# A decoder layer whose second-phase weights wait on a store: other places for two weight tiles and one raw tile

## The chip, the cores and the metric

The kernel runs on one core of a Trainium2 chip. The metric is the device time of one execution in microseconds. It is written in a tile language: the program names tiles from pools, and a planner sets the order of the instructions in each engine's queue, gives the tiles their places and adds the waits. Each engine then works through its own queue in that order.

## The reference

One hybrid decoder layer on 1024 tokens of width 1024, in float32:

```
h = x + W_out( concat[ NSA attention, retention ] )     # both read rmsnorm(x) @ W_in
y = h + W_down( relu(rmsnorm(h) @ W_up)^2 )             # W_up 1024 x 4096, W_down 4096 x 1024
```

Only the last line matters here. All products keep full float32 accuracy by splitting each operand into a rounded high part and the remaining low part; a product is three TensorE products (high x high, high x low, low x high).

## The kernel before

The last part of the kernel computes the line with W_up and W_down by a block scheme with seven products in place of eight (a Winograd-like scheme): weights and activations are cut into two by two blocks, and sums of blocks are multiplied.

**First phase** (`up(p)`, lines 1097 to 1187, p = 0 to 15). Each p is a pair of 128-wide slices of the 4096. It forms seven products (named by the weights 11, 12, S2, S1, S3, S4, 22) and from them the blocks u11, u12, u22, u21 after relu and square, in temporary tiles of the pool `fp`, tag `tmp`, 11 places of 2 KB per partition. From those it makes seven sums, kept as split tiles (`keep`, line 1117: k0, k5, k3, k4, k2, k1, k6 in that order). For p up to 14 a kept tile lies in one of the places hac2 to hac7 (hac4 to hac7 for p = 13 and 14) and is stored to HBM as dU by a DMA that POOL issues; for p = 15 it stays in SBUF. The pair's weight operands lie in the places wo8 to wo11, for p = 14 in hac0 to hac2, for p = 15 in hac0 to hac3.

**Second phase** (lines 1303 to 1400). Eight groups g of two pairs each, and in each group two halves c of the output columns. For each (g, c) seven products n, each of 2 x 6 TensorE products of 128 x 512: in the first block (g = 0, c = 0) in the order 0, 3, 5, 2, 4, 1, 6. Group 0 is pairs 0 and 15. The weights of W_down are loaded raw, four sums are made of them by VectorE, and each of seven is split: ScalarE casts the high part (line 1005), VectorE subtracts to get the low part (line 175).

**The first weights** (`first_w`, lines 1264 to 1291) are prepared beside pair 15. `first_w` is a generator; it is moved one step on before pair 15's sums and at each of the yields of `up(15)`: its raw tiles take wo8 to wo11; after u11 is kept, it splits weights 0, 3 and 5 into `tmp` tiles; after u12 and u22 are copied out of PSUM (lines 1169 and 1172), weights 2 into hac6 and 1 into hac2; after the sums, 4 into hac7 and 6 into hac3. In the call put(n, i) a number i means the place hac i, and none means two `tmp` tiles. hac2 and hac3 last held weights of pair 15; hac6 and hac7 last held k4 and k2 of pair 14.

**The later weights** (`later_w`, lines 1322 to 1329) take raw tiles wq (14 KB per partition) and split tiles wh and wl, two of each, from the pool `fd`, which is opened when the pools of the first phase are closed and lies over their places. A tile of `fd` waits for the last users of what lay there. From low to high: the "T1" and "T4" blocks, "12"/"T3", "22", then the raw tiles of the first weights (wo8 to wo11), small temporaries, and the "11", "21" and "T2" blocks. Tiles of `fd` are laid out in the order in which the program names them first: wh, wl, wh, wl, then wq, then eleven places u10, u9, u8, u7, u0 to u6 of 4 KB each, into which the kept tiles are loaded back from dU. SP issues those loads, POOL those of wq.

The planner plans with its own times; an instruction whose tile has no free place yet is passed over and others of its engine come first. Places of one tag are given out in the order in which the tiles are named.

Of the kernel before, what the change touches and what calls it, by code (L numbers as in the profile page):

```python
# [11 lines left out]
F32 = mybir.dt.float32  # L12
F32R = mybir.dt.float32r
# [88 lines left out]
def hybrid_layer(ctx, tc, xT, x, wfm, wv, vecs, pe, w1, w2, w_out, w_up, w_down,  # L102
# [901 lines left out]
    def split(to, raw):  # L1004
        nc.scalar.copy(to[0], raw)  # L1005
        sub_lo(to[1], raw, to[0])
# [42 lines left out]
    places = {"raws": raws, "ma": ma}  # L1049
# [197 lines left out]
    def load_w(g, c, parts, q=nc.gpsimd):  # L1247

        cols = slice(256 * c, 256 * c + 256)
        for k, p in enumerate(pairs[g]):  # L1250
            for i, to in enumerate(parts):
                q.dma_start(to(k), w_down[2 * p + i].rearrange("p (h n) -> p h n", h=2)[:, :, cols])  # L1252

    def sums_w(b):

        minus(b[3], b[4], b[6], ALU.add)
        minus(b[2], b[3], b[0])
        minus(b[4], b[0], b[4])
        minus(b[5], b[1], b[2])
# [4 lines left out]
    def first_w():  # L1264

        t = [fw.tile([128, 2, 2, 256], F32, name=f"wq0{i}", tag=f"wo{8 + i}") for i in range(4)]
        load_w(0, 0, [lambda q: t[0][:, :, q], lambda q: t[1][:, :, q]], nc.sync)
        b = {n: t[i][:, j].rearrange("p q n -> p (q n)")
             for i, ns in enumerate(((0, 4), (1, 6), (3, 2), (5,))) for j, n in enumerate(ns)}
        yield  # L1270

        def put(n, i=None):
            if i is None:
                w0[n] = [fp.tile([128, 512], F32R, name=f"w0{n}{j}", tag="tmp", bufs=11) for j in range(2)]
            else:
                to = hs.tile([128, 2, 512], F32R, name=f"w0{n}", tag=f"hac{i}")
                w0[n] = [to[:, 0], to[:, 1]]
            split(w0[n], b[n])

        sums_w(b)  # L1280
        for n in (0, 3, 5):
            put(n)
        yield
        put(2, 6)
        put(1, 2)
        yield
        put(4, 7)
        put(6, 3)
        yield
        yield  # L1290

    sums, w0 = norm(), {}
    for p in range(1, NU):
        fetch_up(p + 1)
        ahead = first_w() if p == NU - 1 else itertools.repeat(None)
        next(ahead)
        sums_up(p)
        for _ in up(p):
            next(ahead)
        first_up(p + 1)  # L1300
        if p >= 4:
            next(sums, None)
    ups.close()

    with ExitStack() as s1:
        fd = s1.enter_context(tc.tile_pool(name="fd", reuse_waits="tile", bufs=1))
        dx, dy, dz = Ring("DX"), Ring("DY"), Ring("DZ")

        def wide(n, g, c, dtype=F32R):
            return fd.tile([128, 7, 2, 256], dtype, name=f"{n}_{g}{c}", tag=n if n == "wq" else f"{n}{c}")  # L1310


        parts_w = {(g, c): [wide(n, g, c) for n in ("wh", "wl")] for g, c in ((1, 0), (0, 1))}
        raw_w = {(0, 1): wide("wq", 0, 1, F32)}
        places["fd"] = fd
        early = {k: fd.tile([128, 2, 512], F32R, name=f"u{'0' if k < 7 else '1'}{k}", tag=f"u{k}")
                 for k in (10, 9, 8, 7, 0, 1, 2, 3, 4, 5, 6)}
        for _ in range(11):
            next(spots)
        early = [early[k] for k in range(11)]  # L1320
# [53 lines left out]
        for g in range(NG):  # L1374
            for c in range(2):
# [10 lines left out]
                for n in ORDER if g or c else (0, 3, 5, 2, 4, 1, 6):  # L1386
                    ps = y if n in (3, 5) else z if n == 1 else x
                    for j in range(2):
# [3 lines left out]
                        else:  # L1392
                            k = 2 * c + j
# [119 lines left out]
```

## Time and profile before

| | us |
|---|---|
| median of three runs | 1305.87 |
| the three runs | 1301.57, 1305.87, 1306.34 |
| profiled execution | 1302.99 |
| its span | 1301.2 |
| TensorE busy | 1239.2 |
| VectorE busy | 997.7 |
| ScalarE busy | 684.2 |

The times stand on a scale from the span's start. The first phase of the last part runs from about 670 to 974 us, the second to the end. PE is TensorE, DVE VectorE, ACT ScalarE, POOL GpSimd, SP SyncE. A TensorE product's shown duration (0.39 us) overlaps the next one: what counts is the distance of starts. Tile names in rows leave numbers out: "w<-wq" is a cast of one of the first weights, "u<-px" the copy of u12, "k<-u" a kept tile, "dU<-k" its store.

### The profile page before, as it was taken

How to read it: one execution, taken by the hardware profiler on the slowest of the kernel's cores; microseconds unless marked ns; L12 is line 12 of the kernel's file. 1: busy time of each engine (PE TensorE's matmuls, PEld its weight loads, DVE VectorE, ACT ScalarE, POOL GpSimd, SP SyncE). 2: the span in 40 equal slices, each digit the busy share in tenths (PEclk: the TensorE clock that was granted, in tenths of full speed). 3: DMA queues.
4: the chain of work that ended last, by engine and by line, in shares of the span. 5: the costliest groups of instructions: out<-in, count | busy, mean ns of one | idle time of the engine just before them, and what ended most of it. 6: DMA issues, size and time to landing. Idle time of an engine off the chain costs nothing.

```text
span 1301.2 us, 19827 instructions
## 1 busy us (share of the span) xinstructions
PE 1239.2 (95%) x6682; PEld 1059.8 (81%) x6682; DVE 997.7 (77%) x2185; ACT 684.2 (53%) x1348; POOL 366.5 (28%) x551
## 2 busy tenths in 40 slices
PE   7999999799999999889989999999979999999898
PEld 6888878799999988677767888888767878878786
DVE  7685874588779886577798788887764687787887
ACT  7424412467788775454677787777664322112220
POOL 0344424555566463122101111211110111101010
PEclk9999999899999999999999999999989999999899
DMA  6477569212321531981326777777772578766563
GB/s 231 139 226 212 156 191 321 98 58 74 108 76 63 210 106 40 267 228 66 122 82 250 275 274 259 291 254 269 278 283 108 224 282 306 268 222 251 214 251 121
DMA packets 98805, 252.30 MB, mean 194 GB/s; under 512 B 12640, under 2 KB 30432, under 8 KB 98704
## 3 DMA queue, kind: packets, MB, share of 16 engines
q1 hardware_dynamic: 69488, 150.05, 35.3%
q0 software_dynamic: 29216, 100.98, 20.2%
q8 instruction: 53, 0.87, 0.3%
q14 instruction: 48, 0.39, 0.1%
HBM read 162.19 MB, written 88.74 MB: 193 GB/s over the span
## 4 chain that ended last, share of the span: by engine, by line
PE 32%; issue 12%; DVE 8%; DMA 5%; POOL 3%; ACT 2%; SPq 0%; POOLq 0%; DVEq 0%; ACTq 0%
PE dx L1348 4%; PE dx L1349 4%; PE dx L1347 4%; POOL dU L166 2%; PE dy L1347 2%; PE dy L1348 2%; PE dy L1349 2%; PE px L1106 2%; PE px L1108 2%; DMA rg<-dRG 2%; PE px L1107 2%; DVE y L1357 1%; PE dz L1347 1%; PE dz L1348 1%; PE dz L1349 1%
## 5 line engine op out<-in xcount | busy, mean ns | idle before, releaser
L166 POOL DMA_DIRECT2D dU<-k x105 | 56.0, 533 | 250.4 <-DVE k L175 250.1
L1252 POOL DMA_DIRECT2D wq<-in_w_down x60 | 42.5, 714 | 259.9 <-DVE wl L175 244.2
L1005 ACT CAST wh<-wq 128x1536 fp32r<-128x1536 f32 (+1 forms) x30 | 50.8, 1699 | 118.2 <-DVE wq L1009 99.2
L1347 PE MATMUL dx<-u,wh 128*128 128x512 f32 x232 | 90.0, 394 | 3.1 <-ACT wh L1005 1.6
L1348 PE MATMUL dx<-u,wl 128*128 128x512 f32 x232 | 91.2, 393 | 0.6 <-DVE wl L175 0.6
L175 DVE TENSOR_TENSOR tl<-pt,th 128x512 fp32r<-128x512 f32 (+2 forms) x136 | 80.2, 597 | 14.6 <-ACT th L784 14.0
L1349 PE MATMUL dx<-u,wh 128*128 128x512 f32 x232 | 90.3, 392 | 0.0
L1357 DVE TENSOR_TENSOR y<-dx,y 128x512 f32<-128x512 f32 x90 | 61.3, 687 | 30.9 <-PE dx L1349 28.2
L1005 ACT CAST k<-u 128x512 fp32r<-128x512 f32 x112 | 67.6, 622 | 30.9 <-DVE u L1009 29.2
L175 DVE TENSOR_TENSOR k<-u,k 128x512 fp32r<-128x512 f32 x112 | 76.3, 686 | 6.8 <-ACT k L1005 6.4
L784 ACT CAST th<-pt 128x512 fp32r<-128x512 f32 (+2 forms) x136 | 68.1, 515 | 22.6 <-PE pt L839 20.3
L839 PE MATMUL pt<-ident,p 128*128 128x128 f32 x456 | 71.8, 275 | 0.8 <-DVE sbias L707 0.5
L831 PE MATMUL po<-tl,v 128*128 128x256 f32 (+1 forms) x272 | 70.2, 293 | 0.8 <-DVE tl L175 0.8
L831 PE MATMUL po<-th,v 128*128 128x256 f32 (+1 forms) x272 | 68.6, 274 | 0.1
L1391 ACT COPY dz<-dx 128x512 f32<-128x512 f32 x32 | 18.3, 570 | 95.1 <-PE dx L1349 95.1
L775 POOL TENSOR_SCALAR p<-p,rs 128x896 f32<-128x896 f32 (+3 forms) x64 | 48.0, 749 | 48.3 <-DVE rs L773 20.5
L175 DVE TENSOR_TENSOR wl<-wq,wh 128x1536 fp32r<-128x1536 f32 (+1 forms) x30 | 60.3, 2017 | 0.4 <-ACT wh L1005 0.4
L759 ACT ACTIVATE p<-p,mn 128x896 f32<-128x896 f32 (+3 forms) x64 | 49.8, 778 | 13.7 <-DVE mn L752 13.0
L839 PEld LDWEIGHTS pt<-ident,p 128*128 128x128 f32 x456 | 52.4, 140 | 5.0 <-DVE tl L175 1.4
L1106 PE MATMUL px<-bhT,wS 128*128 128x512 f32 x120 | 47.7, 398 | 8.9 <-ACT u L1169 8.9
L1347 PEld LDWEIGHTS dx<-u,wh 128*128 128x128 f32 x232 | 43.8, 189 | 14.1 <-DVE y L1357 3.1
L831 PEld LDWEIGHTS po<-tl,v 128*128 128x128 f32 x272 | 51.5, 189 | 2.1 <-DVE tl L175 1.4
(514 smaller groups left out, 4306.7 us busy)
## 6 DMA issues: line engine op xcount, KB each, us to landing
dU<-k POOLq DMA_DIRECT2D x105, 512.0 KB, 3.6
u<-dU SPq DMA_DIRECT2D x105, 512.0 KB, 6.9
raw<-in_w_up SPq DMA_DIRECT2D x32, 512.0 KB, 4.3
wq<-in_w_down POOLq DMA_DIRECT2D x60, 256.0 KB, 5.1
xraw<-in_xT SPq DMA_DIRECT2D x16, 256.0 KB, 5.2
w1r<-in_w SPq DMA_DIRECT2D x32, 128.0 KB, 3.7
dQ<-stg_Q POOLq DMA_DIRECT2D x8, 512.0 KB, 5.6
q<-dQ SPq DMA_DIRECT2D x64, 64.0 KB, 2.4
```

The costliest lines, as they stand in the source:

```text
L166: return (q or nc.sync).dma_start(dst.bitcast(F32), src.bitcast(F32)).ins
L175: eng.tensor_tensor(lo, src, hi.bitcast(F32), op=ALU.subtract)
L759: nc.scalar.activation(buf[:, :n], buf[:, :n], AF.Exp, scale=-1.0, bias=mn[:, u, fin:fin + 1], accum_out=sm[:, 0, u, 0:1])
L784: nc.scalar.copy(th[:, :w], pt[:, :w])
L831: mm = nc.tensor.matmul(po[:, cs], vals[g, kt // 4][:, kt % 4, br], q[:, o:o + 128 * len(us)], start=False, stop=end and q is parts[1])
L839: nc.tensor.transpose(pt[:, o:o + 128], res[u][0][:, c:c + 128], ident)
L1005: nc.scalar.copy(to[0], raw)
L1106: nc.tensor.matmul(ps, wh[:, cs], bh, start=first and m == 0, stop=False, skip_group_check=not first)
L1347: nc.tensor.matmul(ps, wh[:, q, cs], u[:, 0], start=first and q == 0, stop=False, skip_group_check=not first)
L1348: nc.tensor.matmul(ps, wl[:, q, cs], u[:, 0], start=False, stop=False, skip_group_check=not first)
L1349: nc.tensor.matmul(ps, wh[:, q, cs], u[:, 1], start=False, stop=q == 1, skip_group_check=not first)
L1357: nc.vector.tensor_tensor(y, ps, y, op=ALU.add)
```

## The change

In `first_w` weights 2 and 4 are split into `tmp` tiles instead of hac6 and hac7, and the split of 4 is named one step earlier, behind that of 2. In the second phase the raw tile wq is named third of the rest, behind u10 and u9, where it was named first; so these two move 14 KB down and wq 8 KB up.

```
-        put(2, 6)
+        put(2)
+        put(4)
         put(1, 2)
         yield
-        put(4, 7)
         put(6, 3)
...
-        raw_w = {(0, 1): wide("wq", 0, 1, F32)}
-        places["fd"] = fd
-        early = {k: fd.tile([128, 2, 512], F32R, name=f"u{'0' if k < 7 else '1'}{k}", tag=f"u{k}")
-                 for k in (10, 9, 8, 7, 0, 1, 2, 3, 4, 5, 6)}
+        places["fd"], early, raw_w = fd, {}, {}
+        for k in (10, 9, 8, 7, 0, 1, 2, 3, 4, 5, 6):
+            if k == 8:
+                raw_w[0, 1] = wide("wq", 0, 1, F32)
+            early[k] = fd.tile([128, 2, 512], F32R, name=f"u{'0' if k < 7 else '1'}{k}", tag=f"u{k}")
```

## Rows read from the trace of the kernel before

**Rows 1.** The page: span, busy time of the engines.
```profile
span 1301.2 us, 19827 instructions
...
PE 1239.2 (95%) x6682; PEld 1059.8 (81%) x6682; DVE 997.7 (77%) x2185; ACT 684.2 (53%) x1348; POOL 366.5 (28%) x551
```

**Rows 2.** Waits of TensorE, whole run: us in total, times, longest us.
```profile
PE px L1106 <- ACT u L1169: 8.9, 2, 8.2
...
PE dy L1347 <- DVE y L1357: 3.1, 1, 3.1
...
PE dy L1347 <- ACT y L1355: 1.4, 1, 1.4
```

**Rows 3.** The chain that ended last, 940 to 1000 us: start, us, what.
```profile
954.85 8.31 DMA dU<-k
```

**Rows 4.** Timeline of ScalarE, 953 to 964.5 us: start, us, engine, line, operation.
```profile
957.20 1.12 ACT L1005 CAST w<-wq 128x512 fp32r<-128x512 f32 x2
958.23 0.63 ACT L1115 ACTIVATE u<-u 128x512 f32<-128x512 f32 x1
958.76 0.60 ACT L1005 CAST w<-wq 128x512 fp32r<-128x512 f32 x1
959.27 0.62 ACT L1005 CAST k<-u 128x512 fp32r<-128x512 f32 x1
959.79 0.62 ACT L1005 CAST w<-wq 128x512 fp32r<-128x512 f32 x1
963.18 0.62 ACT L1005 CAST w<-wq 128x512 fp32r<-128x512 f32 x1 [2.78 <-DMA dU<-k]
963.71 0.58 ACT L1169 COPY u<-px 128x512 f32<-128x512 f32 x1
```

**Rows 5.** Timeline of TensorE, 955 to 969 us.
```profile
955.53 0.39 PE L1107 MATMUL pz<-bl,w 128*128 128x512 f32 x1
955.76 0.39 PE L1108 MATMUL pz<-bh,w 128*128 128x512 f32 x1
964.34 0.79 PE L1106 MATMUL px<-bhT,wS 128*128 128x512 f32 x1 [8.19 <-ACT u L1169]
...
968.35 0.44 PE L1106 MATMUL px<-bhT,wS 128*128 128x512 f32 x1
```

**Rows 6.** Two other holes of TensorE; stretches beside them, third column from the end: granted clock.
```profile
238.80 0.58 PE L347 MATMUL a_RVA<-wh_RVA,xhi 128*128 128x256 f32 x1 [4.47 <-ACT gRG L356]
...
673.60 0.51 PE L1106 MATMUL pz<-bh,w 128*128 128x512 f32 x1 [2.69 <-ACT pz L1160]
...
238.00:245.00 7.00, 5.49 (x24) 5.19 (x24) 5.01 (x14) 2.04 (x5) 5.30 (x7) 0.51 0.31 95
...
675.00:678.00 3.00, 3.00 (x9) 2.32 (x8) 3.00 (x6) 1.84 (x3) 0.55 (x1) 0.50 0.67 274
```

**Rows 7.** Timeline of POOL, 950 to 1000 us.
```profile
972.05 2.88 POOL L1252 DMA_DIRECT2D wq<-in_w_down  x4 [14.65 <-PE py L1108]
999.64 0.71 POOL L1252 DMA_DIRECT2D wq<-in_w_down  x1 [24.70 <-DVE wl L175]
```

**Rows 8.** Stretches around these loads: the last two columns are DMA share and GB/s.
```profile
963.00:972.00 9.00, 7.66 (x25) 6.18 (x26) 1.98 (x3) 4.07 (x7) 0.00 (x0) 0.70 1.03 420
...
978.00:990.00 12.00, 10.56 (x47) 8.44 (x46) 3.95 (x7) 4.43 (x9) 0.00 (x0) 1.00 0.01 1
```

**Rows 9.** Timelines of ScalarE, VectorE and TensorE in the second phase's first block.
```profile
974.74 0.60 ACT L1114 ACTIVATE u<-px 128x512 f32<-128x512 f32 x1
...
991.81 2.01 DVE L1009 TENSOR_TENSOR wq<-wq 128x512 f32<-128x512 f32 x3
...
994.94 1.75 DVE L175 TENSOR_TENSOR wl<-wq,wh 128x1536 fp32r<-128x1536 f32 x1
...
995.97 0.61 PE L1347 MATMUL dx<-u,wh 128*128 128x512 f32 x2
...
996.75 0.50 PE L1348 MATMUL dx<-u,wl 128*128 128x512 f32 x1 [0.16 <-DVE wl L175]
```

## The prediction

> **What bounds the kernel now.** I read the page first [rows 1]: TensorE is busy for 95% of the span, so the time falls only where TensorE waits or runs slowly. The waits of TensorE over the whole run [rows 2] name the largest such place in one row: 8.2 us at one time, a product into px that waits for ScalarE's copy of u (line 1169). It is in the last pair of the first phase (p = 15). The chain that ended last [rows 3] says what stood behind it: from 954.85 us, for 8.31 us, the store of a kept product into dU; when it lands, ScalarE's cast of a first weight w starts. ScalarE's timeline [rows 4] shows the queue: the cast that waited 2.78 us for "DMA dU<-k" and directly behind it the copy of u for which TensorE waits. A queue in order holds the copy back, though the copy has nothing to do with the store. In the code the waiting cast is put(4, 7): its target hac7 was last the source of the store of k2 of pair 14. Of the two casts "x2" at 957.20 one is put(2, 6), into hac6, the source of k4's store, which has landed by then.
>
> TensorE's timeline [rows 5] gives the price. Products run 0.23 us apart (955.53, 955.76); the last one before the hole ends at 956.15, the next begins at 964.34. Nine products then take 964.34 to 968.35, 4.01 us, where 9 x 0.227 = 2.04 us is the usual time: 1.97 us more, because the granted clock is at 1.2 of its 2.4 GHz after the hole (mean 0.70 from 963 to 972 [rows 8]). The place costs 8.19 + 1.97 = 10.2 us in all.
>
> **The change part by part.**
>
> *put(2) and put(4) go to temporaries.* No instruction goes or comes; two casts and two subtracts get other targets. A "tmp" place is given out in the order in which the program names the tiles (11 places). Before, the six halves of weights 0, 3, 5 are named ahead of u12 and u22, and weights 2 and 4 used hac places, so that they could slip ahead of u12 on ScalarE. Now 2 and 4 are named behind u12 and u22 in the same ring and must come later. So ahead of the u12 copy there are left, from 957.20 on: the cast of 0, the square of u11, the cast of 3, the cast of k0, the cast of 5. ScalarE steps 0.52 us from one to the next when it waits for nothing (958.76, 959.27, 959.79 in [rows 4]). The copy starts at 957.20 + 5 x 0.52 = 959.80 instead of 963.71: 3.91 us earlier. That is the wait with its wake-up, 963.18 - (959.79 + 0.52) = 2.87 us, and two casts that now stand behind the copy, 1.04 us. TensorE resumes at about 960.43, and the hole is 4.28 us instead of 8.19. It does not close: the five instructions, and the relu of u11 ahead of them, remain. Bounds: -2.87 us if both casts are still ahead, -8.19 if the planner finds a way to copy u12 at once. I take -3.91.
>
> *The clock.* Holes of 4.47 us (ending at 238.80) and 2.69 us (ending at 673.60) are each in the neighbourhood of a stretch at half the granted clock: 238 to 245 at 0.51, 675 to 678 at 0.50 [rows 6]. A hole of 4.28 us lies between these two. Beside the first the slow stretch covers some 6 us of work (a loss of 3.0), beside the second 3 us (1.5); now it is 1.97. So bounds +1.0 and -0.5, and -1.97 if no slow stretch came; I take 0: a hole that is only halved still pays.
>
> *What is now short: the ring.* Pair 15 needs u11, u12, u22, u21 and ten halves of weights, 14 tiles in 11 places. The halves of 4 get their places only when u11 and u12 are used up, and u21 one when the first product of the second phase (n = 0) has used weight 0. Times, all moved by 3.9: pair 15's last product ends at about 970.6, n = 0 takes 12 x 0.227 = 2.7 us, so the relu of u21 starts at about 973.5, against 974.74 before [rows 9]. It was late already: nothing is lost against it. k1 and k6, made from u21, are first read at n = 1 and n = 6, the last in the order 0, 3, 5, 2, 4, 1, 6, and even n = 4 is 4 x 2.7 us away. Weight 4's split ends at about 975, six microseconds before n = 4. What can move is TensorE's wait of 1.4 us for the copies "y" (the row dy <- ACT y in [rows 2]), which stand on ScalarE behind the cast of k6. With u21 later the cast of k6 comes behind them: a gain up to 1.4; one more cast (weight 4) stands there: a loss up to 0.6, or 1.2 with its subtract's delay. I take -0.7.
>
> *The later weights' raw tile moves.* With u10 and u9 named first, wq takes 8 KB further on: it leaves the last quarter of the "22" blocks and lies over the raw tiles of the first weights. Its four loads on POOL (issued from 972.05 on, 2.88 us [rows 7]) wait for TensorE's S4 product and the raw splits before; now for the subtract of weight 4, at about 975. POOL has nothing else to issue until 999.64, so nothing is queued behind them. They are used by VectorE's sums from 991.81 on, and TensorE's first product with the later weights is at 995.97 [rows 9]; moved by 3.9 this is 987.9 and 992.1. The DMA engines are full until 972 (share 1.03) and idle from 978 on (0.01) [rows 8]: before, all four had landed 6 us after the first issue; so now at 981, 7 us ahead of the sums. Cost 0, bounds 0 and the shift that rival C prices. The Trainium skill ("DMA: Bandwidth & Descriptors", section "Issuing engines are not separate DMA queues") says that transfers started by different engines end up on the same 16 DMA engines and interleave; by that rule a load that meets SP's loads of the kept tiles could take the 8.3 us of the store in [rows 3] from its last issue and land at 986, 2 us ahead of the sums instead of 7, the sum still being what it is and rival C nearer. The share of 0.01 in [rows 8] speaks against such a meeting. u10 and u9 now wait for TensorE's S4 product and are read two groups later: 0.
>
> *Behind it* TensorE is dense: of the waits in [rows 2] the second phase has 3.1 us and smaller ones, so what is gained here is kept to the end unless the planner, which orders every engine's queue anew for the whole second phase, draws it otherwise. That I cannot read from a trace; the size of one such redrawn place is the row dy <- DVE y: 3.1 us and its slow clock.
>
> **Sum.** -3.9 + 0 - 0.7 + 0 = -4.6 us. The profiled execution took 1302.99 us (span 1301.2 and 1.8 around it): 1298.4. The median of the runs, 1305.87, is 2.9 above the profiled one; from it 1301.3. I name the middle, 1299.8.
>
> **The rivals.**
> A. *The hole closes.* ScalarE copies u12 ahead of the weights, and the slow clock goes with it: -10.2 us, from the middle base of 1304.4 to 1294.2. For it: the product that it copies stands ahead of pz's in TensorE's queue, and pz's is through at the hole's start. Against it: the order of the names, which keeps six halves of weights ahead of u12.
> B. *Nothing is gained.* The ring of 11 is too short in practice: the planner puts u21's relu ahead of the cast of k3 on ScalarE, both stand until n = 0 is through, and n = 3 waits for relu, square, cast [rows 4] and subtract (2.01 us for three in [rows 9]), 0.6 + 0.6 + 0.6 + 0.7 = 2.5 us, and the y copies 1.4 more: -3.9 + 3.9 = 0, 1304.4. For it: 14 tiles in 11 places. Against it: k3 is made by a subtract that waits neither for u21 nor for n = 0.
> C. *Slower.* The raw tile of the later weights comes free too late. The load needs 2.9 us to issue and about 3 to land, the sums to the first product 995.97 - 991.81 = 4.2, the first subtract 1.75 [rows 9]: some 12 us from issue to use. The second block needs it at 992.1, so up to an issue at 980 nothing shows, and each us beyond is one on the path. If weight 4's places come free only at the end of the first block (7 x 2.7 us after 970.6, at 989.6), TensorE stands until 1001.6, 9.5 us, and the sum is -3.9 + 9.5 = +5.6, with a slow clock of 1.5 to 3 behind the hole: +7 to +8.6, about 1312. For it: the last reader of that place is the very weight that now waits for a place. Against it: two places come free at about 973 with u11 and u12.
> D. *The planner's new order* makes or removes a later hole such as that of 3.1 us, with 1.5 to 3 us of slow clock: 5 to 6 us either way, 1294 or 1305.
>
> **How the numbers follow.** Likeliest 60%, A 9%, B 13%, C 5%, D 13%, half to each side. The likeliest's own range is -2 to -8 us (the bounds of the hole and the clock, and runs that lie 5 us apart among themselves), so a good fourth of it is beyond 0.5%, which is 6.5 us and about what a measurement here can tell from no change. Faster: 0.26 x 60 + 9 + 6 = 31%; slower: C and a little of D, 6%; the same: 63%. The range is 1293 to 1306.5: A and the good half of D at its low end, B and the bad half of D at its high end; C and the tails are left out.
>
> **What would show it.** Right: no cast of w on ScalarE waits for "DMA dU<-k"; the copies of line 1169 and 1172 follow directly on the cast of weight 5; TensorE's hole before S3 is 4 to 4.5 us and still has half a clock behind it; wq's load is issued near 975 and no product waits for wh or wl more than the 0.2 us of before. Wrong: a hole under 2 or over 6 us; a new wait of TensorE on k1, k3, w or wh in the 30 us behind pair 15; a change of the waits after 1000 us larger than that of the hole.

## The result, and the profile after

The changed kernel took 1295.48 us (median of 16 runs, 1292.81 to 1301.60), the kernel before beside it on the same chip 1303.88 us (16 runs, 1300.80 to 1307.58): a ratio of 0.9942, interval 0.9930 to 0.9954, so about 7.6 us less. The time lies inside the range of 1293.0 to 1306.5 and 4.3 us below the 1299.8 named. Of the three classes the one with the largest chance (within 0.5%, 63%) did not come; faster by over 0.5% (31%) did, by little. Run twice more, the changed kernel gave 0.9958 [0.9943, 0.9974] and 0.9948 [0.9930, 0.9966]: whether the gain is over 0.5% is not settled by these, that there is a gain is.

The profiled execution of the changed kernel took 1300.51 us, 5 above its median: its total says little here, and the places inside it say much. Its span is 1298.7 us. From the page, the busy times as in [rows 1]:

```profile
PE 1240.7 (96%) x6682; PEld 1062.0 (82%) x6682; DVE 997.8 (77%) x2185; ACT 684.1 (53%) x1348; POOL 366.0 (28%) x551
```

The work is the same; what went is waiting. TensorE's waits after (us in total, times, longest), against [rows 2]; the second phase's lines stand one further down in the code:

```profile
PE px L1106 <- ACT u L1169: 4.9, 2, 4.3
...
PE dy L1348 <- DVE y L1358: 3.1, 1, 3.1
...
PE dy L1348 <- DMA u<-dU: 2.1, 1, 2.1
```

The wait on line 1169's copy is 4.3 us instead of 8.2, the one on the copies y (1.4 us) has no row any more, that on VectorE's y is unchanged, and there is a new one on a load of a kept tile. ScalarE's timeline after shows the queue of [rows 4] without the store:

```profile
958.30 0.59 ACT L1114 ACTIVATE u<-pz 128x512 f32<-128x512 f32 x1
958.79 0.61 ACT L1005 CAST w<-wq 128x512 fp32r<-128x512 f32 x1
959.30 0.63 ACT L1115 ACTIVATE u<-u 128x512 f32<-128x512 f32 x1
959.83 0.60 ACT L1005 CAST w<-wq 128x512 fp32r<-128x512 f32 x1
960.34 0.62 ACT L1005 CAST k<-u 128x512 fp32r<-128x512 f32 x1
960.86 0.62 ACT L1005 CAST w<-wq 128x512 fp32r<-128x512 f32 x1
961.38 0.58 ACT L1169 COPY u<-px 128x512 f32<-128x512 f32 x1
961.85 0.59 ACT L1172 COPY u<-py 128x512 f32<-128x512 f32 x1
962.33 0.63 ACT L1005 CAST w<-wq 128x512 fp32r<-128x512 f32 x1
```

Between the relu of u11 and the copy stand exactly the five instructions of the prediction (the casts of 0, 3 and 5, a square, a kept tile's cast), none of them with a wait; weight 2's cast comes behind both copies. TensorE's timeline after, the place of [rows 5], and under it stretches of the same trace (columns: length, busy time and count of PE, PEld, DVE, ACT, POOL, then granted clock, DMA share, GB/s):

```profile
957.35 0.39 PE L1108 MATMUL pz<-bh,w 128*128 128x512 f32 x1
962.01 0.50 PE L1106 MATMUL px<-bhT,wS 128*128 128x512 f32 x1 [4.27 <-ACT u L1169]
...
965.53 0.63 PE L1106 MATMUL px<-bhT,wS 128*128 128x512 f32 x1
```

```profile
962.00:966.00 4.00, 3.99 (x11) 3.15 (x12) 1.05 (x2) 0.96 (x2) 0.00 (x0) 0.58 1.02 412
...
970.00:980.00 10.00, 10.00 (x46) 8.29 (x45) 6.60 (x11) 7.24 (x14) 2.88 (x4) 1.00 0.73 277
980.00:990.00 10.00, 10.00 (x45) 8.29 (x45) 7.50 (x11) 6.10 (x7) 0.00 (x0) 1.00 0.11 36
```

The hole is 4.27 us, and half a clock still follows it (0.58). From 970 to 990 us TensorE now has no gap at all, where before it stood 1.44 us in 12 (978 to 990, [rows 8]). Behind pair 15, the later weights' load, their sums and the copies y, from the timelines of POOL, VectorE and ScalarE:

```profile
976.14 2.88 POOL L1252 DMA_DIRECT2D wq<-in_w_down  x4 [17.12 <-DMA u<-dU]
992.56 2.86 POOL L1252 DMA_DIRECT2D wq<-in_w_down  x4 [13.55 <-DVE wl L175]
```

```profile
974.86 0.69 DVE L175 TENSOR_TENSOR w<-wq,w 128x512 fp32r<-128x512 f32 x1
...
984.21 2.61 DVE L1009 TENSOR_TENSOR wq<-wq 128x512 f32<-128x512 f32 x4
```

```profile
977.29 0.57 ACT L1356 COPY y<-dy 128x512 f32<-128x512 f32 x1
...
978.28 0.59 ACT L1356 COPY y<-dy 128x512 f32<-128x512 f32 x1
...
979.94 0.62 ACT L1005 CAST k<-u 128x512 fp32r<-128x512 f32 x1 [1.07 <-DVE u L1009]
```

The load goes out at 976.14 (the prediction: near 975), 0.59 us after the end of weight 4's subtract (974.86 and 0.69); it is the same 0.59 us in again, put_only and put_again, though the row names a kept tile's load as the last thing waited for. The four loads land 3.2 to 5.2 us after their issue, the last at 983.52. The sums start at 984.21 and run in one piece of four; before they started at 991.81 as three, with one more at 994.34. The cast of the last kept tile (979.94) stands behind the copies y. Before it stood ahead of them, on ScalarE:

```profile
979.90 0.62 ACT L1005 CAST k<-u 128x512 fp32r<-128x512 f32 x1 [1.35 <-DVE u L1009]
...
980.95 1.06 ACT L1355 COPY y<-dy 128x512 f32<-128x512 f32 x2
```

TensorE's own order in the first block changed too. Before, product n = 5, whose dy waits for the copies y, came directly behind n = 3; now n = 2 (into dx) stands between them. TensorE's timeline after, the starts of n = 2 and of n = 5:

```profile
977.34 0.39 PE L1348 MATMUL dx<-u,w 128*128 128x512 f32 x1
...
980.06 0.39 PE L1348 MATMUL dy<-u,w 128*128 128x512 f32 x1
```

**Where the time went.** To compare kernels without the noise of whole executions I count TensorE's 6682 products in order of start from 0, and take the distance between the starts of two numbers. Product 5301 is the last before the hole, 5302 the first behind it; up to 5350 lies the stretch with the slow clock and pair 15's end, up to 5372 the place of the wait for y, up to 5470 the rest of the first block and the start of the second. Which product bears a number can differ between kernels from 5362 on, where the orders part. All traces of this study, in us:

```
kernel        5301-5302  -5350  -5372  -5470 | 5301-5470 | 5470-last
before             8.58  12.92   6.71  23.35 |     51.56 |    289.09
order_only         8.30  13.61   6.64  23.35 |     51.90 |    287.91
changed            4.66  12.61   4.99  22.21 |     44.47 |    292.10
again              4.66  13.59   4.99  22.21 |     45.45 |    291.23
again_2            4.66  12.35   4.99  22.21 |     44.21 |    291.13
put_only           4.66  13.51   4.99  22.21 |     45.37 |    290.53
put_again          4.66  12.62   4.99  22.21 |     44.48 |    289.00
w4_only            5.18  13.05   6.37  23.33 |     47.93 |    292.43
w4_again           5.18  13.66   6.24  23.34 |     48.42 |    290.60
w2_only            8.42  12.52   5.64  22.22 |     48.79 |    294.01
late_names         2.07  11.01   4.99  22.21 |     40.28 |    288.22
late_put           2.07  11.01   4.99  22.21 |     40.28 |    287.71
```

The first two rows have the same order on every engine, the old one; their mean is 51.73. The five rows with the changed order have a mean of 44.80: 6.9 us less; the five timed ratios (0.9942 to 0.9958) make 5.5 to 7.6 us of 1304. Of these 8.44 - 4.66 = 3.8 is the hole, 13.27 - 12.94 = 0.3 the clock, 6.68 - 4.99 = 1.7 the wait for y, 23.35 - 22.21 = 1.1 the second block's start. The last column, from 5470 on, scatters by 3 us among the five executions with the changed order: that is why single totals mislead. Its mean for them is 290.80, 2.3 above the 288.50 of the first two rows, so the traces give some of the gain back. One part of that comes in all five: a new wait at product 5851 for a kept tile's load, 0.16 to 0.97 us, where the 100 products from 5800 on take 23.44 to 23.93 us instead of the 22.67 of the first two rows. In the changed kernel's first profile:

```profile
1091.38 0.50 PE L1348 MATMUL dx<-u,wh 128*128 128x512 f32 x1 [0.62 <-DMA u<-dU]
```

On the other side a wait of 0.92 us at product 5676, which the profile of before has, is gone. How much of the 2.3 us is the order and how much the execution, five traces against two do not tell.

### The profile page after: what moved, and what is told of

Same layout as the page of the kernel before. It is cut to its first block, busy times and chain, and to the rows that moved or that the text cites. A ratio compares the mean times of both kernels' runs of the same rounds, so it can differ in the third digit from the quotient of the medians.

```text
span 1298.7 us, 19825 instructions
## 1 busy us (share of the span) xinstructions
PE 1240.7 (96%) x6682; PEld 1062.0 (82%) x6682; DVE 997.8 (77%) x2185; ACT 684.1 (53%) x1348; POOL 366.0 (28%) x551
## 4 chain that ended last, share of the span: by engine, by line
PE 40%; DVE 10%; DMA 6%; ACT 4%; issue 3%; POOL 0%; SPq 0%; DVEq 0%; ACTq 0%; POOLq 0%
PE dx L1350 3%; PE dx L1349 3%; PE dx L1348 3%; PE px L1106 3%; PE px L1108 3%; PE px L1107 3%; PE dy L1349 2%; PE dy L1348 2%; PE dy L1350 2%; PE py L1106 2%; PE py L1107 2%; PE py L1108 2%; DMA u<-dU 1%; DVE y L1358 1%; DMA raw<-in_w_up 1%
```

## The experiments

My theory was that the hole's change is the forecast one, that the raw tile's place is worth nothing, and that what came on top is the planner's redrawn order of the first blocks. The rivals: the raw tile's place gave the extra gain, or the extra was noise of the executions, or weight 4's move alone carries all.

**again, again_2: the changed kernel, unaltered.**

> The changed kernel once more, for a second trace and a direct comparison with the halves. Theory 1 (the hole): the gain is made between 955 and 1000 us, some 7 us there (hole 8.2 to 4.3 us, the 1.4 us wait for the y copies gone, the second block's start 0.9 us closer), and the wait of 2.1 us for a load u<-dU near 1017 us in the first trace of the changed kernel is chance and absent here. Ratio to the kernel before 0.994. Rival (the new order and place cost something later): the 2.1 us wait is there again, in the same place.

> The changed kernel once more, for the wait of 2.13 and 1.76 us of a product on a kept tile's load (u<-dU) near 1015 us, which both its profiles have had and no profile of the kernels with the raw tile at its old place. If it comes with the raw tile's new place: 1.5 to 2.3 us again. If it is one execution's DMA traffic: it is as likely to be gone. Ratio 0.994 to 0.996 by either; hole 4.27.

Measured: 1295.65 us, 0.9958 [0.9943, 0.9974], and 1296.71 us, 0.9948 [0.9930, 0.9966]. The hole is 4.27 us and the two stretches behind it 4.99 and 22.21 us in all three traces: the extra gain repeats. The new wait on a load near 1015 us was expected to be absent in again and came, by 1.8 us; in again_2 it is 0.34 us (at 1014.66). TensorE's timelines, first of the changed kernel's first profile, then of again:

```profile
1018.85 0.50 PE L1348 MATMUL dy<-u,wh 128*128 128x512 f32 x1 [2.13 <-DMA u<-dU]
```

```profile
1014.49 0.50 PE L1348 MATMUL dy<-u,wh 128*128 128x512 f32 x1 [1.76 <-DMA u<-dU]
```

**put_only, put_again: the weights' places changed, the raw tile where it was.** Against the kernel before:

```
-        put(2, 6)
+        put(2)
+        put(4)
         put(1, 2)
         yield
-        put(4, 7)
         put(6, 3)
```

> Weights 2 and 4 in temporaries as in the change, raw tile wq where it was. Every engine has the same order as in the changed kernel; only places and waits differ. Theory 1: the same time as the changed kernel, 0.994 +- 0.001, hole 4.3 us; the place of the raw tile is worth nothing. Rival (the place): part of the gain beyond the forecast 4.6 us belongs to wq, u10 and u9, so this one is 3 to 4 us slower than the changed kernel (0.997).

> Weights 2 and 4 in temporaries, raw tile as before, a second time, for its trace and time. Theory (the wait of 2 us near 1015 us comes with the raw tile's new place): absent again, ratio 0.994. Rival (chance of the transfers): it is there this time, ratio the same.

Measured: 1295.57 us, 0.9952 [0.9933, 0.9971], and 1296.92 us, 0.9954 [0.9941, 0.9968]: the same as the changed kernel. Every engine's order is the changed kernel's, and the four columns of the table agree with its rows. Neither trace has the wait on a load near 1015 us.

**order_only: the raw tile's place alone.** Against the kernel before:

```
-        raw_w = {(0, 1): wide("wq", 0, 1, F32)}
...
+        for k in (10, 9, 8, 7, 0, 1, 2, 3, 4, 5, 6):
+            if k == 8:
+                raw_w[0, 1] = wide("wq", 0, 1, F32)
```

> Only the raw tile's place as in the change; weights 2 and 4 in hac6 and hac7 as before. Every engine has the same order as in the kernel before. Theory 1: 0 +- 1 us (0.999 to 1.001), hole 8.2 us. Rival (the place): 3 to 4 us faster (0.997).

Measured: 1302.71 us, 1.0005 [0.9988, 1.0022]. Its order is that of before on every engine. ScalarE's timeline still has the wait for the store, as [rows 4]:

```profile
965.31 0.62 ACT L1005 CAST w<-wq 128x512 fp32r<-128x512 f32 x1 [2.50 <-DMA dU<-k]
965.84 0.58 ACT L1169 COPY u<-px 128x512 f32<-128x512 f32 x1
```

With put_only this settles that half of the diff: the place of the raw tile moves nothing, neither with the other half nor without it.

**w4_only, w4_again: only weight 4 leaves the store's places.** Against the kernel before:

```
         put(2, 6)
+        put(4)
         put(1, 2)
         yield
-        put(4, 7)
         put(6, 3)
```

> Only weight 4 goes to temporaries, named behind weight 2, which stays in hac6; raw tile as before. The order of the engines stays that of the kernel before but for a few instructions (TensorE 12 of 6641), so that the hole is changed without the new order of the second phase. Theory 1 in its narrow form (only the hole counts): one more cast ahead of the copy than in the changed kernel, hole 4.8 us, gain 3.4 us (0.9974); the wait of 1.4 us for the y copies stays. Rival (the new order of the first blocks counts as much): the gain of the changed kernel is not reached by some 3 to 4 us; if the hole alone were all, this one would be 0.5 us behind the changed kernel.

> Only weight 4 in temporaries, a second time. Hole 4.8 us and the wait for the y copies 1.1 us again; between the hole's start and the second block 3.5 us ahead of the kernel before where the changed kernel is 6 to 7 us ahead; ratio 0.997, behind the changed kernel by 0.1 to 0.3%.

Measured: 1297.91 us, 0.9968 [0.9954, 0.9981], and 1300.56 us, 0.9971 [0.9957, 0.9986]. ScalarE's timeline in w4_only:

```profile
959.84 1.13 ACT L1005 CAST w<-wq 128x512 fp32r<-128x512 f32 x2
960.86 0.63 ACT L1115 ACTIVATE u<-u 128x512 f32<-128x512 f32 x1
961.39 0.61 ACT L1005 CAST w<-wq 128x512 fp32r<-128x512 f32 x1
961.90 0.62 ACT L1005 CAST k<-u 128x512 fp32r<-128x512 f32 x1
962.42 0.62 ACT L1005 CAST w<-wq 128x512 fp32r<-128x512 f32 x1
962.94 0.58 ACT L1169 COPY u<-px 128x512 f32<-128x512 f32 x1
```

No wait for the store; one cast more ahead of the copy ("x2", weight 2's among them); a hole of 4.79 us where the changed kernel has 4.27: the 0.52 us of one step. But the wait of TensorE for the copies y stays, 1.1 us in w4_only's list of waits:

```profile
PE dy L1347 <- ACT y L1355: 1.1, 1, 1.1
```

and the second block's start is that of before (23.33). TensorE's order is that of before throughout. The cast of the last kept tile did move here, behind the first of the two copies:

```profile
979.97 0.57 ACT L1355 COPY y<-dy 128x512 f32<-128x512 f32 x1
981.03 0.62 ACT L1005 CAST k<-u 128x512 fp32r<-128x512 f32 x1 [0.49 <-DVE u L1009]
981.55 0.58 ACT L1355 COPY y<-dy 128x512 f32<-128x512 f32 x1
```

So the place of that cast is worth 0.3 to 0.4 us of the wait (1.09 and, in w4_again, 0.93 us, against 1.44 and 1.32 with the old order). The hole alone is worth 3.3 us; with the 0.4 less at the wait for y it is 3.5 us in the table and about 0.3% timed. What the changed kernel has beyond that hangs on weight 2.

**w2_only: only weight 2 leaves the store's places.** Against the kernel before:

```
-        put(2, 6)
+        put(2)
         put(1, 2)
         yield
         put(4, 7)
```

> Only weight 2's target is changed (a temporary instead of the place that the store of k4 reads); weight 4 still goes into the place that the store of k2 reads, the raw tile stays where it was. All theories: the copy still stands behind weight 4's cast and so behind the store, the hole before S3 stays 7.9 to 8.2 us. Theory (weight 2's place alone makes the planner run n = 2 ahead of n = 5 and pull the second block's products forward): no wait of TensorE for the copies y; from product 5350 to 5372 5.0 us instead of 6.7, from 5372 to 5470 22.2 instead of 23.35; 2.8 us gained, ratio 0.9978. Rival (the new order comes only when both weights have left the store's places): 6.6 and 23.3 us as before, ratio 1.000. Second rival (weight 2 now comes behind u12 on ScalarE and is late because of the store ahead of it): a new wait on weight 2, ratio above 1.001.

Measured: 1303.30 us, 1.0002 [0.9983, 1.0021]. The theory was right about the place and wrong about the time. Weight 4's cast is still held by the store, and the hole is 8.03 us; but the second block's start falls to 22.22 us and the wait for y is gone from the list (5350 to 5372 takes 5.64, with a 0.36 us wait for a copy of dz in its stead): 2.9 us below the mean of the old order up to product 5470, of which 0.75 is the slow stretch, that scatters by more. So weight 2's place alone redraws the first blocks. It also shows what took the wait for y away: n = 2 stands ahead of n = 5 as in the changed kernel, while the cast of the last kept tile is still ahead of both copies:

```profile
981.03 0.62 ACT L1005 CAST k<-u 128x512 fp32r<-128x512 f32 x1 [1.00 <-DVE u L1009]
...
982.08 1.06 ACT L1355 COPY y<-dy 128x512 f32<-128x512 f32 x2
```

The whole of it is given back later (294.01 in the last column against 288.50). Here the planner drew the later groups anew as well, up to 1230 us. TensorE's timeline in w2_only, waits that no trace of before or of the changed kernel has in this size:

```profile
1190.03 0.69 PE L1347 MATMUL dy<-u,wh 128*128 128x512 f32 x1 [2.13 <-ACT wh L1005]
...
1229.70 0.50 PE L1347 MATMUL dy<-u,wh 128*128 128x512 f32 x1 [3.63 <-DVE y L1357]
```

and the stretch behind the first, whose clock is at 0.53 where it is 1.00 in the kernel before:

```profile
1190.00:1193.60 3.60, 3.32 (x7) 2.33 (x8) 3.60 (x4) 0.09 (x1) 0.00 (x0) 0.53 0.15 23
```

This is rival D, both halves of it, in one kernel. The changed kernel has less of the bad half: in its program TensorE's order differs from before in 432 positions, all in the first five of the eight groups, and from there on is the same; the wait at product 5851 lies in that stretch.

**late_names: the halves of 0, 3 and 5 named behind u12 and u22 too.** Against the changed kernel:

```
         sums_w(b)
+        yield
         for n in (0, 3, 5):
             put(n)
-        yield
         put(2)
```

> The changed kernel with weights 0, 3 and 5 named one step later, behind u12 and u22: on ScalarE the two copies follow directly on the relu of u11. Theory 1 (the five instructions ahead of the copy are what is left of the hole): hole 4.27 - 5 x 0.52 = 1.7 us, no slow clock behind it (1.5 us more), so 4 us faster than the changed kernel, 0.991 of the kernel before. Rival (the second block is now limited by the DMA engines, which are full from 990 to 1016 us): TensorE gets to the same loads 4 us earlier and waits there for u<-dU by as much, so nothing or at most 1 to 2 us is left, 0.994.

Measured: 1291.60 us against 1303.25, 0.9910 [0.9896, 0.9925]. It beats both kernels. ScalarE's timeline in late_names, then TensorE's at the hole, then a stretch from the hole's end on (columns as above):

```profile
954.05 0.59 ACT L1114 ACTIVATE u<-pz 128x512 f32<-128x512 f32 x1
954.54 0.58 ACT L1169 COPY u<-px 128x512 f32<-128x512 f32 x1
```

```profile
953.10 0.39 PE L1108 MATMUL pz<-bh,w 128*128 128x512 f32 x1
955.17 0.50 PE L1106 MATMUL px<-bhT,wS 128*128 128x512 f32 x1 [1.68 <-ACT u L1169]
```

```profile
955.00:964.00 9.00, 8.83 (x39) 7.32 (x40) 6.65 (x11) 7.68 (x15) 0.00 (x0) 1.00 1.01 370
```

The copy follows the relu at once. The hole is 1.68 us, and the clock stays at 1.00 behind it: the slow stretch's 1.3 to 2.6 us (12.35 to 13.59 in the table against 11.01) go with it. In all 51.73 - 40.28 = 11.5 us up to product 5470, and the timed ratio keeps them (0.9910 is 11.7 us of 1303). Behind 5470 the planner's order is not the changed kernel's: the wait at product 5851 is gone, and the last column (288.22, and 287.71 in late_put) is that of the old order again.

**late_put: late_names with the raw tile where it was.** Against late_names:

```
+        raw_w = {(0, 1): wide("wq", 0, 1, F32)}
...
-            if k == 8:
-                raw_w[0, 1] = wide("wq", 0, 1, F32)
```

> The same with the raw tile where it was in the kernel before (the order of every engine is that of late_names). Theory (the place is worth nothing): the same time as late_names, within 0.1%. Rival (the place costs the wait of some 2 us for u<-dU near 1015 us, which both traces of the changed kernel have and the one trace with only the put change has not): 2 us faster than late_names, and no such wait.

Measured: 1291.99 us, 0.9910 [0.9895, 0.9925], the table's row that of late_names: the raw tile's place is worth nothing here either.

## Why the prediction was right, and where it fell short

**The hole (-3.91): right.** 4.28 us were forecast and 4.27 came, by the same five instructions. Both parts of the term are seen apart: w4_only takes the store away (hole 4.79) and the changed kernel also moves one more cast behind the copy (4.27). w2_only shows that the cast moved alone is worth nothing as long as the store decides.

**The clock (0): right, within its scatter.** Behind the holes of 4.3 and 4.8 us the stretch to product 5350 takes 12.35 to 13.66 us, behind those of 8 us 12.52 to 13.61: the slow clock costs the same after half a hole. It is gone behind the hole of 1.68 us in both late_names and late_put; from which length on, no run here tells.

**The raw tile (0) and rival C: right, and refuted.** The issue at 976.14 and the sums at 984.21 leave no trace in TensorE's time, and three comparisons without the move (put_only with put_again against the changed kernel, order_only against before, late_put against late_names) show no difference in the time. The prediction had the load landed at 981, and at 986 if it met SP's loads; it landed at 983.52, 0.7 us ahead of the sums instead of 7. In again and put_only it landed 1.8 and 2.2 us ahead of them, so the sums did not start on its landing. The Trainium skill ("DMA: Bandwidth & Descriptors", section "Issuing engines are not separate DMA queues") says that DMAs of different engines interleave on the same 16 DMA engines. These loads do not test it: SP's last load ahead of them had landed at 976.04, SP issued its next one at 992.27, and the DMA share from 980 to 990 is 0.11.

**The wait for y (-0.7) and the planner's new order (left open, priced at 0 in the sum): this step failed.** The wait went whole, 1.7 us with its wake-up, beyond the lower bound of -1.4, and not for the reason given. That reason, the kept tile's cast coming behind the copies, is worth 0.3 to 0.4 us in w4_only and w4_again, where TensorE's order is the old one. In w2_only the cast stays ahead of both copies, and the wait is gone all the same: n = 2 now runs ahead of n = 5, 2.7 us of products in which the copies are made. This half I had left out as not to be read from a trace. The planner also forms the later weights' sums in one piece earlier and draws products of the second block ahead of the first block's last ones; this takes away 1.1 us of small waits (0.37 and 0.16 with their wake-ups, [rows 9] shows the second). Together 2.8 us instead of 0.7. w4_only, without the new order, and w2_only, with it and without the shorter hole, show that it comes from weight 2's place. Up to product 5470 the sum is then -6.9 instead of -4.6. It should have stood in the sum as a term of its own: the waits of 1.4, 0.37 and 0.16 us in the first block were all in the trace, and a draw that removes them was as possible as one that adds some. That the time still fell inside the range is in part luck: the range held it because rival D, a redrawn order, stood in it at even chances either way, not because the sum was right.

**The base.** The middle between the profiled execution and the median of three runs, 1304.4, was good: 16 runs gave 1303.88.

**Rivals.** A did not come in the change. late_names comes near it: the hole and the slow clock together give 8.6 us there (8.44 - 2.07 and 13.27 - 11.01), with 1.68 us of the hole left, where A priced all of it at 10.2; the rest of the 11.5 us is the planner's order (1.7 and 1.1). B is refuted: no product waits for weight 3 or 0. D came with its good side in the changed kernel, at less than the 5 to 6 us it was priced at, and with its bad side in w2_only.

**What stays open.** Whether the waits of 2.13 and 1.76 us on a kept tile's load have to do with the raw tile's new place. Together with the 0.34 us of again_2 such a wait came in all three profiles of the changed kernel and in none of put_only and put_again, but also not in late_names, which has the new place; the times with and without it cannot be told apart.

## What to carry to other kernels

Where TensorE waits for one small instruction, list what stands ahead of it in its engine's queue, and ask of each why it is there; here places given out in the order of naming decided it, and naming six more tiles later took off another 4.5 us. Here the hole that was only halved still paid for the slow clock behind it, so the last microseconds of it were the dearest. A planner that redraws a queue can win and lose as much as the edit: compare traces product by product over the stretch concerned and behind it, and then the timed medians, to see whether the gain is kept. And a wait that goes as forecast may have gone for another reason: one kernel with each cause alone tells them apart.

## What the runs showed of the hardware

Loads that are under way together land late. From 990 to 1015 us, in the changed kernel's first profile, the DMA share was 0.81. A kept tile's load issued at 998.62 landed after 3.4 us, one of the same size issued at 1007.74, with five others still on their way, after 11.1 us, at 1018.80, and the product that read it waited until 1018.85.

Short holes are followed by a slow clock in some executions only. A hole near 930 us, ahead of all that the change touches, was 1.79 us in the changed kernel's first profile, and the clock was at 0.50 behind it; in put_only it was 1.77 us, and the clock stayed at 1.00. TensorE's timeline and a stretch of the changed kernel, then the same two views of put_only:

```profile
931.32 0.50 PE L1106 MATMUL py<-bhT,wS 128*128 128x512 f32 x1 [1.79 <-ACT wS L1005]
```

```profile
931.90:935.30 3.40, 3.40 (x9) 2.65 (x9) 3.37 (x7) 0.95 (x2) 0.48 (x1) 0.50 0.97 394
```

```profile
927.99 0.50 PE L1106 MATMUL py<-bhT,wS 128*128 128x512 f32 x1 [1.77 <-ACT wS L1005]
```

```profile
928.00:932.00 4.00, 4.00 (x18) 3.23 (x19) 3.96 (x8) 2.02 (x4) 0.99 (x2) 1.00 0.96 392
```

Such stretches make up part of the few microseconds by which single executions of one kernel differ; how large a part was not counted.
